# A matmul with subtraction on one core: 16 rows to a partition, another list of transfers, and eleven pairs of tiles transposed on VectorE

## The chip, the core and the metric

The kernel runs on one core of a Trainium2 chip. The metric is the device time in microseconds (us). The kernel before takes 211.34 us (median of eight runs, 210.97 to 211.55).

## What is computed

```python
# x: (16, 512, 1024), weight: (1024, 768), sub_value: (16, 512, 768), all float32
out = (np.matmul(x, weight) - sub_value).astype(np.float32)
```

Flattened, x has 8,192 rows of 1,024 numbers, and output and sub_value have 8,192 rows of 768.

## The kernel before

**Tiles.** The rows are worked in 64 m tiles of 128 rows. A tile doesn't hold 128 rows that follow each other: with `S = 8`, a group of 1,024 rows gives each of the 128 partitions a run of eight rows that lie together in memory, and m tile `mi` is row `mi % 8` of every run of group `mi // 8`. A transfer of n tiles of one group so moves, for each partition, one run of n rows: n x 4,096 bytes of x, or n x 3,072 bytes of sub_value or output.

**Rings.** x lands in a ring of 16 tiles (`x_ring`), sub_value in a ring of 32 (`so_ring`). The result is written over sub_value in place and stored from there. The weight comes in four chunks of 256 of its rows, each through two slots of `so_ring` (slots 24 to 31), from where VectorE (DVE) casts it to float16 (L112).

**Transfers.** All are issued by SyncE (SP), in the order of the list `TRANSFERS`: (kind, first tile, number of tiles), with x, w, s (sub_value) and o (output). `issue()` (L91) takes the head of the list as soon as, in the program's order, what it needs has been written down: for x, the casts of the tiles whose slots it takes; for s, the stores that free its slots; for o, the subtractions. On the chip SP then waits at each issue for those instructions or transfers to have ended, and what is behind in the list waits with it. In the trace the ninth issue also waits for the first transfer to land, the tenth for the second, and so on.

**The work of a tile.**

- ScalarE (ACT) casts x to float16: L135, or L132 for tiles of a pair that DVE will transpose.
- Transpose, by one of two ways. On TensorE (PE): four transposes against the identity (L144; two float16 numbers travel as one float32), then a copy out of PSUM by ACT (L151). On DVE, for the pairs that begin at a tile in `ON_DVE`: 16 stream transposes of 32 x 256 for a pair (L165), no PE and no copy.
- PE: sixteen matmuls of 128 x 128 by 384 columns (L177), into one of three PSUM buffers.
- DVE subtracts sub_value and writes the result (L189, `finish`), which frees the PSUM buffer.

**Order.** Written out by hand. The head (L214 to L242) works tiles 0 to 2 chunk by chunk as the weight arrives, with filler matmuls on zeros between (`idle`, L205). Then the loop over `mi` (L246): tile `mi`'s matmuls, with the PE transposes of tile `mi + 2` between them, then the casts of tiles that are due (four tiles ahead, or seven for a DVE pair), then `finish(mi)`, then up to four waiting DVE transposes. The 16 transposes of a pair join the waiting ones six tiles before the pair and so are spread over four tiles.

```python
    for mi in range(HEAD, n_mt):
        t = mi + TA
        tr = transposes(t) if t < n_mt and t - t % 2 not in ON_DVE else []
...
        finish(mi)
        if mi + LEAD_DVE - 1 in ON_DVE:
            waiting += transposes_dve(mi + LEAD_DVE - 1)
        for f in waiting[:PER]:
            f()
```

Of the kernel before, what the change touches and what calls it, by code (L numbers as in the profile page):

```python
# [10 lines left out]
F32 = mybir.dt.float32  # L11
F16 = mybir.dt.float16

S = 8
NX, NSO = 16, 32
TA = 2
CA = 2
LEAD_DVE = 7
PER = 4
HEAD = 3  # L20
ON_DVE = frozenset(range(18, 60, 6))

TRANSFERS = [
    ('x', 0, 1), ('w', 0, 1), ('x', 1, 1), ('w', 1, 1), ('x', 2, 1), ('w', 2, 1),
    ('w', 3, 1), ('x', 3, 2), ('s', 0, 1), ('x', 5, 3), ('s', 1, 3), ('x', 8, 3),
    ('s', 4, 4), ('x', 11, 5), ('s', 8, 8), ('x', 16, 8), ('x', 24, 3), ('s', 16, 8),
    ('x', 27, 5), ('o', 0, 8), ('s', 24, 8), ('x', 32, 8), ('s', 32, 8), ('o', 8, 8),
    ('x', 40, 8), ('s', 40, 8), ('x', 48, 8), ('o', 16, 8), ('o', 24, 8), ('s', 48, 8),
    ('x', 56, 8), ('s', 56, 8), ('o', 32, 8), ('o', 40, 8), ('o', 48, 8), ('o', 56, 4),
    ('o', 60, 2), ('o', 62, 1), ('o', 63, 1),  # L30
]


# [1 line left out]
def kernel(  # L35
# [20 lines left out]

    x_s = x_flat.rearrange("(s p j) k -> s p j k", p=P, j=S)
    sub_s = sub_flat.rearrange("(s p j) n -> s p j n", p=P, j=S)
    out_s = out_flat.rearrange("(s p j) n -> s p j n", p=P, j=S)
    w_c = weight.rearrange("(c p r) n -> c p r n", p=P, r=2)  # L60

    def rows(view, mi, n):
        return view[mi // S][:, mi % S : mi % S + n]

# [26 lines left out]
    def issue():  # L91
        while todo:
# [24 lines left out]
            here = ring[:, at % size : at % size + n]  # L117
            there = view[at // S][:, at % S : at % S + n]
            if kind == "o":
# [4 lines left out]
    def cast(mi):  # L124
        assert mi in done["x"]
        done["cast"].add(mi)
        x_in = x_ring[:, mi % NX]
        first = mi - mi % 2
        if first in ON_DVE:
            if mi == first:  # L130
                x16_t["pair", mi] = x16p_pool.tile([P, 2, K], F16, name="x16p_tile")
            keep(nc.scalar.copy(out=x16_t["pair", first][:, mi - first], in_=x_in))  # L132
        else:
            x16_t[mi] = x16_pool.tile([P, K], F16, name="x16_tile")
            keep(nc.scalar.copy(out=x16_t[mi], in_=x_in))  # L135
        issue()


    def transposes(mi):
        def one(c):  # L140
            def f():
                if c == 0:
                    ps_t[mi] = psum_t_pool.tile([P, K], F16, name="psum_t")
                keep(nc.tensor.transpose(  # L144
                    ps_t[mi].bitcast(F32)[:, c * P : (c + 1) * P],
                    x16_t[mi].bitcast(F32)[:, c * P : (c + 1) * P],
                    ident,
                ))
                if c == n_c - 1:
                    xt_t[mi] = xt_pool.tile([P, K], F16, name="xt_tile")  # L150
                    keep(nc.scalar.copy(out=xt_t[mi], in_=ps_t.pop(mi)))  # L151
                    x16_t.pop(mi)
            return f
        return [one(c) for c in range(n_c)]

    def transposes_dve(mi):

        x16 = x16_t.pop(("pair", mi)).bitcast(F32).rearrange("p j (c q) -> p (j c) q", c=n_c)
        xt_p = xtp_pool.tile([P, 2, K], F16, name="xtp_tile")
        xt_t[mi], xt_t[mi + 1] = xt_p[:, 0], xt_p[:, 1]  # L160
        xt = xt_p.bitcast(F32).rearrange("p j (c m) -> p (j c) m", c=n_c)

        def one(a, b):
            def f():
                keep(nc.vector.transpose(  # L165
                    xt[b * Q : (b + 1) * Q, :, a * Q : (a + 1) * Q],
                    x16[a * Q : (a + 1) * Q, :, b * Q : (b + 1) * Q],
                ))
            return f
        return [one(a, b) for a in range(P // Q) for b in range(P // Q)]  # L170
# [14 lines left out]
    def finish(mi):  # L185
        assert mi in done["s"]
        done["finish"].add(mi)
        o = so_ring[:, mi % NSO].rearrange("p (h n) -> p h n", h=2)
        keep(nc.vector.tensor_tensor(  # L189
            out=o, in0=po_t.pop(mi)[:, :, :NS], in1=o, op=mybir.AluOpType.subtract  # L190
        ))
        issue()
# [10 lines left out]
    def idle(n):  # L203
        for _ in range(n):
            keep(nc.tensor.matmul(idle_o[:, 0], idle_w, idle_x, start=True, stop=True))  # L205

    def lead(mi):
        return LEAD_DVE if mi - mi % 2 in ON_DVE else TA + CA

# [1 line left out]
        for f in transposes(mi):  # L211
            f()

    idle(13)  # L214
    cast(0)
    transpose_tile(0)
    idle(5)
# [28 lines left out]
# [3 lines that stand above are left out]
        for c in range(n_c):  # L249
# [6 lines left out]
# [3 lines that stand above are left out]
# [34 lines left out]
```

## Time and profile before

| | before |
|---|---|
| median of 8 runs | 211.34 us |
| the profiled execution | 211.03 us |
| its span | 209.2 us |
| granted TensorE clock, mean | 0.998 |
| PE busy | 198.3 us (95%) |
| DVE busy | 114.1 us (55%) |
| ACT busy | 112.8 us (54%) |
| PE waits in all, longest releaser | 2.7 us on the cast (L135) |
| last subtraction ends | 205.1 us |

The span runs from the first to the last instruction of the program; the device time has some 1.8 us more. Times of events are counted from the span's start. Busy shares say how long an engine had an instruction in work, not which engine sets the end: for that one looks at what each stage waits for. The DMA row of the page is the mean busy share of the 16 DMA engines that carry every transfer. A transfer's time to landing runs from its issue on SP to its last byte's completion, and so holds the time that it stands behind earlier transfers.

### The profile page before, as it was taken

The numbers are of one execution on the slowest core, as the hardware profiler recorded it, in microseconds if no ns is written. First come the engines' busy times: TensorE is split into PE (matmuls) and PEld (weight loads), VectorE is DVE, ScalarE is ACT, GpSimd is POOL, SyncE is SP. The second block draws the span as 40 slices with busy tenths as digits, with TensorE's granted clock in tenths as the row PEclk, the third lists the DMA queues.
The fourth block names the chain that finished last, engine by engine and source line by source line (L and its number), as shares of the span: only waits on it lengthen the run. The fifth ranks groups of instructions, "written<-read, shape, count | busy, mean of one in ns | idle before, by whom it ended". The sixth has DMA issues, their size and how long they took to land.

```text
span 209.2 us, 2967 instructions
## 1 busy us (share of the span) xinstructions
PE 198.3 (95%) x1249; PEld 130.4 (62%) x1249; DVE 114.1 (55%) x186; ACT 112.8 (54%) x115; POOL 0.7 (0%) x6
## 2 busy tenths in 40 slices
PE   7997799999989999999999999999999999999990
PEld 3464467667656566667667666667666766767650
DVE  0342044206149759929947955982993795333231
ACT  3555665675496193555727629456473750765410
POOL 1000000000000000000000000000000000000000
PEclk9999999999999999999999999999999999999999
DMA  6999999999999999999999999999999999999994
GB/s 220 420 429 422 427 431 436 441 436 439 387 451 418 436 442 407 464 420 418 440 415 440 434 423 443 432 415 421 432 442 445 420 421 423 431 423 428 432 390 186
DMA packets 5629, 87.22 MB, mean 417 GB/s; under 512 B 624, under 2 KB 624, under 8 KB 2032
## 3 DMA queue, kind: packets, MB, share of 16 engines
q1 hardware_dynamic: 5616, 87.03, 97.8%
q8 instruction: 10, 0.16, 0.3%
q14 instruction: 3, 0.02, 0.0%
HBM read 61.87 MB, written 25.17 MB: 416 GB/s over the span
## 4 chain that ended last, share of the span: by engine, by line
PE 68%; DMA 20%; ACT 4%; DVE 3%; SPq 2%; issue 1%
PE psum_o L177 60%; DMA x_ring<-in_x_dram 20%; PE psum_t L144 8%; ACT x_tile L135 2%; DVE xtp_tile L165 2%; ACT xt_tile L151 1%; DVE so_ring L189 1%; SPq L110 1%; SPq L122 1%; ACT x16p_tile L132 0%
## 5 line engine op out<-in xcount | busy, mean ns | idle before, releaser
L177 PE MATMUL psum_o<-w_sb,xt_tile 128*128 128x384 f16 x800 | 145.7, 326 | 1.2 <-ACT xt_tile L151 1.0
L177 PEld LDWEIGHTS <-xt_tile 128*128 128x128 f16 x800 | 78.2, 98 | 41.0 <-ACT xt_tile L151 1.8
L189 DVE TENSOR_TENSOR so_ring<-psum_o,so_ring 128x768 f32<-128x768 f32 x64 | 60.7, 956 | 61.4 <-PE psum_o L177 41.2
L151 ACT COPY xt_tile<-psum_t 128x1024 f16<-128x1024 f16 x50 | 50.6, 1012 | 73.6 <-PE psum_t L144 72.8
L165 DVE STREAM_TRANSPOSE xtp_tile<-x16p_tile 32x256 f32<-32x256 f32 x112 | 48.8, 436 | 18.2 <-ACT x16p_tile L132 16.5
L144 PE MATMUL psum_t<-ident,x_tile 128*128 128x128 f32 x200 | 52.3, 274 | 3.0 <-ACT x_tile L135 2.7
L135 ACT CAST x_tile<-x_ring 128x1024 f16<-128x1024 f32 x50 | 51.6, 1049 | 6.3 <-DMA x_ring<-in_x_dram 6.3
L177 PE MATMUL psum_o<-w_sb,xtp_tile 128*128 128x384 f16 x224 | 42.9, 326 | 0.3 <-DVE xtp_tile L165 0.3
L144 PEld LDWEIGHTS psum_t<-ident,x_tile 128*128 128x128 f32 x200 | 27.7, 141 | 17.0 <-ACT x_tile L135 5.0
L177 PEld LDWEIGHTS <-xtp_tile 128*128 128x128 f16 x224 | 21.8, 98 | 10.4 <-DVE xtp_tile L165 0.7
L132 ACT CAST x16p_tile<-x_ring 128x1024 f16<-128x1024 f32 x14 | 14.6, 1046 | 6.5 <-DMA x_ring<-in_x_dram 6.5
L205 PE MATMUL psum_o<-idle_x,idle_w 128*128 128x512 f16 x25 | 8.8, 508 | 1.3 <-DVE idle_x L200 1.3
L112 DVE CAST w_sb<-so_ring 128x768 f16<-128x768 f32 x8 | 4.1, 556 | 10.6 <-DMA so_ring<-in_weight_dram 10.6
L205 PEld LDWEIGHTS <-idle_w 128*128 128x128 f16 x25 | 3.1, 122 | 4.9 <-issue 3.2
L135 ACT ACT_TABLE_LOAD x1 | 1.3, 1283 | 0.7 <-PEq L277 0.7
L199 DVE MEMSET idle_w<- 128x64 uint32 x1 | 0.1, 112 | 0.8 <-PEq L277 0.8
masks.py:199 POOL TENSOR_SCALAR_AFFINE_SELECT ident<-ident 128x128 f32<-128x128 f32 x1 | 0.3, 292 | 0.1
L200 DVE MEMSET idle_x<- 128x256 uint32 x1 | 0.3, 272 | 0.0
masks.py:197 POOL MEMSET ident<- 128x128 f32 x1 | 0.2, 205 | 0.3 <-POOLq L277 0.3
L277 POOL MEMSET const-bfloat16-1.0<- 128x1 bf16 x1 | 0.1, 101 | 0.0
L277 POOL MEMSET const-uint8-127<- 128x1 uint8 x1 | 0.1, 101 | 0.0
L277 POOL MEMSET const-float32-0.0<- 128x1 f32 x1 | 0.1, 99 | 0.2 <-issue 0.2
(1 smaller groups left out, 0.1 us busy)
## 6 DMA issues: line engine op xcount, KB each, us to landing
so_ring<-in_sub_value_dram SPq DMA_DIRECT2D x7, 3072.0 KB, 24.7
out_dram<-so_ring SPq DMA_DIRECT2D x7, 3072.0 KB, 31.2
x_ring<-in_x_dram SPq DMA_DIRECT2D x5, 4096.0 KB, 22.9
x_ring<-in_x_dram SPq DMA_DIRECT2D x2, 2560.0 KB, 23.1
x_ring<-in_x_dram SPq DMA_DIRECT2D x3, 1536.0 KB, 19.4
so_ring<-in_weight_dram SPq DMA_DIRECT2D x4, 768.0 KB, 8.8
x_ring<-in_x_dram SPq DMA_DIRECT2D x3, 512.0 KB, 6.3
so_ring<-in_sub_value_dram SPq DMA_DIRECT2D x1, 1536.0 KB, 21.8
```

What stands on the lines that cost most here:

```text
L110: keep(nc.sync.dma_start(out=st, in_=w_c[at]))
L112: keep(nc.vector.tensor_copy(out=w_sb[:, at, r], in_=st[:, r]))
L122: keep(nc.sync.dma_start(out=here, in_=there))
L132: keep(nc.scalar.copy(out=x16_t["pair", first][:, mi - first], in_=x_in))
L135: keep(nc.scalar.copy(out=x16_t[mi], in_=x_in))
L144: keep(nc.tensor.transpose(ps_t[mi].bitcast(F32)[:, c * P : (c + 1) * P], x16_t[mi].bitcast(F32)[:, c * P : (c + 1) * P], ident,))
L151: keep(nc.scalar.copy(out=xt_t[mi], in_=ps_t.pop(mi)))
L165: keep(nc.vector.transpose(xt[b * Q : (b + 1) * Q, :, a * Q : (a + 1) * Q], x16[a * Q : (a + 1) * Q, :, b * Q : (b + 1) * Q],))
L177: keep(nc.tensor.matmul(po_t[mi][:, h, :NS], xt_t[mi][:, 2 * P * c + r : 2 * P * (c + 1) : 2], w_sb[:, c, r, h * NS : (h + 1) * NS], start ...
L189: keep(nc.vector.tensor_tensor(out=o, in0=po_t.pop(mi)[:, :, :NS], in1=o, op=mybir.AluOpType.subtract))
L205: keep(nc.tensor.matmul(idle_o[:, 0], idle_w, idle_x, start=True, stop=True))
L277: nc = _bacc.Bacc("TRN2", target_bir_lowering=False, num_devices=1)
```

## The change

Four things in one diff:

- `S` goes from 8 to 16: groups of 2,048 rows, each partition holding a run of 16. Transfers may now be up to 16 tiles long, and their runs up to 49,152 bytes. The rows of one m tile lie 64 KB apart in x instead of 32 KB, in sub_value and output 48 KB instead of 24 KB.
- The list of transfers is another: 34 entries instead of 39. Weight chunk 0 goes first, ahead of x tile 0. Sub_value starts with tiles 0 to 5 in one transfer (before: tile 0, then 1 to 3, then 4 to 7). The stores are of 16, 12, 4, 16, 7, 6, 2 and 1 tiles.
- `ON_DVE` holds eleven pairs, from tile 12 to tile 55, most of them four tiles apart, instead of seven pairs six tiles apart (18 to 55).
- Sixteen filler matmuls instead of 13 before the first cast.

```diff
-S = 8
+S = 16
 NX, NSO = 16, 32
 TA = 2
 CA = 2
 LEAD_DVE = 7
 PER = 4
 HEAD = 3
-ON_DVE = frozenset(range(18, 60, 6))
+ON_DVE = frozenset((12, 16, 20, 24, 28, 32, 38, 42, 46, 50, 54))
 
 TRANSFERS = [
-    ('x', 0, 1), ('w', 0, 1), ('x', 1, 1), ('w', 1, 1), ('x', 2, 1), ('w', 2, 1),
-    ('w', 3, 1), ('x', 3, 2), ('s', 0, 1), ('x', 5, 3), ('s', 1, 3), ('x', 8, 3),
-    ('s', 4, 4), ('x', 11, 5), ('s', 8, 8), ('x', 16, 8), ('x', 24, 3), ('s', 16, 8),
-    ('x', 27, 5), ('o', 0, 8), ('s', 24, 8), ('x', 32, 8), ('s', 32, 8), ('o', 8, 8),
-    ('x', 40, 8), ('s', 40, 8), ('x', 48, 8), ('o', 16, 8), ('o', 24, 8), ('s', 48, 8),
-    ('x', 56, 8), ('s', 56, 8), ('o', 32, 8), ('o', 40, 8), ('o', 48, 8), ('o', 56, 4),
-    ('o', 60, 2), ('o', 62, 1), ('o', 63, 1),
+    ('w', 0, 1), ('x', 0, 1), ('x', 1, 1), ('w', 1, 1), ('x', 2, 1), ('w', 2, 1),
+    ('w', 3, 1), ('x', 3, 3), ('s', 0, 6), ('x', 6, 3), ('x', 9, 7), ('s', 6, 5),
+    ('x', 16, 6), ('s', 11, 5), ('s', 16, 6), ('x', 22, 10), ('x', 32, 4), ('s', 22, 10),
+    ('o', 0, 16), ('x', 36, 4), ('s', 32, 5), ('x', 40, 8), ('s', 37, 11), ('x', 48, 8),
+    ('o', 16, 12), ('o', 28, 4), ('s', 48, 7), ('x', 56, 8), ('s', 55, 9), ('o', 32, 16),
+    ('o', 48, 7), ('o', 55, 6), ('o', 61, 2), ('o', 63, 1),
 ]
...
-    idle(13)
+    idle(16)
     cast(0)
     transpose_tile(0)
```

## The prediction

> **What bounds the kernel now.** I read the 40 slices of the page first, then the DMA queues, the issues with their times to landing, and the chain last.
>
> Page, parts 2 and 3 (busy tenths of the 16 DMA engines, GB/s moved; packets, MB, share):
>
> ```profile
> DMA  6999999999999999999999999999999999999994
> GB/s 220 420 429 422 427 431 436 441 436 439 387 451 418 436 442 407 464 420 418 440 415 440 434 423 443 432 415 421 432 442 445 420 421 423 431 423 428 432 390 186
> ...
> q1 hardware_dynamic: 5616, 87.03, 97.8%
> ```
>
> From the second slice to the last but one the DMA engines never rest, and 87.03 MB is what has to move: x 33.55, weight 3.15, sub_value and output 25.17 each. A landing is the issue time plus the time to landing. The load of m tiles 24-31 of sub_value lands at 87.87, the load of x 32-39 behind it at 97.59: 4.19 MB in 9.72 us, 431 GB/s. That pace holds to the end. The last two stores, from the DMA view of a window around each (KB, us to landing):
>
> ```profile
> out_dram<-so_ring SPq DMA_DIRECT2D x1, 384.0 KB, 4.9
> ```
>
> ```profile
> out_dram<-so_ring SPq DMA_DIRECT2D x1, 384.0 KB, 3.2
> ```
>
> The first is issued at 202.51 and lands at 207.4, the second at 205.11 and 208.3: 0.9 us apart, just the time of its bytes (eight packets of 3,072 bytes an engine, 0.121 us each in the trace's packet records, 0.97). So the last store hardly waited for its late issue; the slowest engine was still behind.
>
> PE looks like the bound too. The chain in order of time ends so:
>
> ```profile
> 198.88 5.21 PE psum_o L177 x32
> 204.12 0.96 DVE so_ring L189
> ```
>
> From 60 us to 204 it is nearly all PE at L177. **Two limits end together**: the data (208.3) and PE, then DVE at L189, then the last store (204.1 + 1.0 + 3.2 = 208.3). A gain must come from both; PE's alone is worth nothing.
>
> **DVE transposes and PE.** From the groups (count, busy us, mean ns):
>
> ```profile
> L165 DVE STREAM_TRANSPOSE xtp_tile<-x16p_tile 32x256 f32<-32x256 f32 x112 | 48.8, 436 | 18.2 <-ACT x16p_tile L132 16.5
> L144 PE MATMUL psum_t<-ident,x_tile 128*128 128x128 f32 x200 | 52.3, 274 | 3.0 <-ACT x_tile L135 2.7
> ```
>
> Eleven pairs for seven take eight m tiles from PE: 32 transposes fewer. One costs PE less than its 274 ns, which overlap: in the chain four matmuls with a transpose begin every 0.76 us, and 36 without take 5.85, or 0.65 for four. So 32 x 0.11 = **3.5 us off PE**; ACT loses 8 copies of 1.012 us (L151), 8.1 us, unneeded there (busy 54%). DVE gains 64 transposes, 28 us. The timeline of DVE shows its pace (start, duration):
>
> ```profile
> 60.08 1.78 DVE L165 STREAM_TRANSPOSE xtp_tile<-x16p_tile 32x256 f32<-32x256 f32 x4 [5.03 <-ACT x16p_tile L132]
> 61.90 0.96 DVE L189 TENSOR_TENSOR so_ring<-psum_o,so_ring 128x768 f32<-128x768 f32 x1
> 62.88 1.78 DVE L165 STREAM_TRANSPOSE xtp_tile<-x16p_tile 32x256 f32<-32x256 f32 x4
> ```
>
> A subtraction and four transposes repeat every 2.80 us. Pairs are now four tiles apart instead of six, so DVE works without pause, 4 x 2.80 = 11.20 us a pair, where PE needs 2 x 3.04 + 2 x 2.60 = 11.28. It fits by 0.08 us; time that DVE loses to a late sub_value tile comes back only at the six-tile step from 32 to 38 and after the last pair.
>
> **The head.** Weight chunk 0 goes ahead of x tile 0 on SP's queue: x 0 lands 0.79 MB / 0.429 = 1.8 us later (4.8 becomes 6.7), and the cast, transposes and first matmuls on ACT and PE move by about 1.1 us. From x 1 on the bytes ahead are the same. The three added fillers cost 0.75 to 1.3 us (0.25 or 0.44 each in the timeline), while PE waits for x 0 anyway. All this is covered: PE must then wait for x 3, now in a transfer of three tiles, until about 18.7 (17.4 before). Next late is sub_value: tiles 0-5 come as one transfer ending at 8.65 MB, where before 8.91 MB had landed at 25.6: about 25.0. The subtraction of tile 0 is done at 26.0, and only then is one of three output banks free for tile 3, which ends at 29.1 instead of 26.7: **+2.4 us on PE**. Later, x 9-15 (13.89 MB) land near 37.2, just in time for the transposes beside tile 7 (38.2). Sub_value 6-10 (15.86 MB) lands at 41.9 and holds DVE 3.7 us, so pair 12's transposes end at 41.9 + 11.2 = 53.1 where tile 12 is due at 52.5: a stall of 0.6. Before, PE lost 2.2 us near 57, 59 and 70, where x 16-23 landed at 56.2, after their casts were due; now x 16-21 land at 49 and x 22-31 at 71, needed by PE at 53 and 76, so these waits go. Beyond this sub_value comes in time or under 1 us late, inside the slack of three banks.
>
> PE's end: 204.1 + 2.4 + 0.6 - 2.2 - 3.5 = 201.4. The last subtraction ends at 202.4, the last store is issued 2.7 us earlier than now. So PE leaves the path; **the DMA engines stay**.
>
> **The transfers.** The packet records give 8 data packets and one of 4 bytes an engine for every transfer (39 x 144 = 5,616). Median durations: 121 ns for 3,072 bytes, 912 for 24,576, 1,213 for 32,768. The slope is 36.7 ns a KB (1,000 bytes), the fixed part 9 ns; the 4-byte packet also takes 9. A transfer thus costs 9 x 9 = 81 ns beyond its bytes, and 34 instead of 39 save 5 x 81 = **0.4 us**. No other fixed cost is seen between transfers: 8 x 1.213 + 0.009 is the 9.71 us that landings are apart.
>
> The page "DMA: Bandwidth & Descriptors" of the Trainium skill (Bandwidth, Measured) gives a fixed cost of about 2 us a DMA; five fewer would then save 10 us, which the back-to-back landings here rule out.
>
> What could leave a DMA engine idle? SP issues in order, and two loads of sub_value wait for a store to land: tiles 32-36 for output 0-15, tiles 48-54 for output 16-27. Queued behind each store is only x 36-39 (2.10 MB, 4.9 us) or output 28-31 (1.57 MB, 3.7 us); before, it was 3.15 to 7.34 MB. An issue needs 4.1 - 1.3 = 2.8 us beside its own bytes (x 0) or 3.2 - 1.0 = 2.2 (the last store). Both are under 3.7, so the cost is nothing; even if the whole 4.1 of x 0 were needed, it would be 0.4. The large x transfer 22-31 waits for the cast of tile 15, which stands behind tile 11's matmuls and so is done near 53.5, while the data queued before it last to 59 (23.33 MB); x 32-35 wait for tile 19's, behind tile 15, near 65.4, against 71 (28.57 MB).
>
> No row has a packet above 32,768 bytes; five transfers now have runs of 33,792 to 49,152. If cut in two, they add at most 5 x 8 x 9 ns = 0.36 us; if not, nothing. I take nothing, as the fixed part is flat from 3,072 to 32,768. No row has rows spaced 64 KB (x) or 48 KB: the spacings of 6 KB (weight), 24 and 32 KB lie on one line within 1%. That bounds it to 1% of 203 us, 2.0 us, either way; I take nothing.
>
> The same page (Latency and other measured facts, on HBM row pitch) speaks against the change: at a pitch of 512 KiB it has 207 GB/s against 214, and half at 4 MiB. It states nothing for 64 KiB; its 3% would be 6 us.
>
> **Sum.** 211.03 of the profiled execution (span 209.2, 1.8 around it) less 0.4 is 210.6; the shown median is 0.3 above that execution, so I set 211.34 - 0.4 = **210.9**. Chance moves it by about as much: the trace holds ten 16 KB instruction fetches of about 1.0 us, each delaying one engine, and one landing's lag of the last engine behind the first grew from 0.93 to 1.69 us at the first of them. Measurement tells 0.2%, 0.42 us, from no change.
>
> **Rivals.**
> - *The saving doesn't show* (0.18): runs are cut (-0.4 + 0.36), or an extra fetch or a store wait gives 0.4 back. 211.3. For it: unseen sizes; against: the flat fixed part.
> - *A fetch misses the slowest engine* (0.07): 0.6 more is saved, 210.3. The first one shows what is at stake.
> - *Wider row spacing slows packets* (0.10), the slower side: in every x, sub_value and output transfer, every 1% is 2.0 us, so that 1% gives 211.34 + 2.0 - 0.4 = 212.9. It decides from 0.4%, 0.8 us. Against it: three spacings on one line.
> - *DVE becomes the bound* (0.05): with 0.08 us to spare a pair, lateness beyond the computed one pushes PE one for one. The store before the last would land near 206.9 and an issue needs 2.8, so the last one may be issued up to 204.1, 1.7 later than computed; 3 us of lateness give 210.9 + 1.3 = 212.2.
>
> **Numbers.** The forecast case has 0.60, from 210.4 to 211.3: 0.40 faster, 0.20 within. Faster: 0.40 + 0.07 = 0.47. Same: 0.20 + 0.18 = 0.38. Slower: 0.10 + 0.05 = 0.15. The range 210.1 to 212.2 takes in the first three cases and the milder part of the last two.
>
> **What would show it.** Right: DMA tenths full to the last slice, 4,896 packets on q1, the chain's last subtraction near 202.4 with the last store's time to landing 2 to 3 us longer, DVE without gaps between 42 and 110 us. Wrong: a slice below 9 near 102 or 152 (store waits), 24 KB packets off 0.912 us (spacing), more than 4,896 packets (cut runs), or PE waiting at L177 for xtp_tile again and again (DVE).

## The result, and the profile after

The changed kernel takes **213.16 us** (median of 11 runs, 212.34 to 215.0) against 211.18 for the kernel before (31 runs beside them): a ratio of 1.0102, with an interval of 1.0087 to 1.0117. It is 1% slower, where 0.2% faster was forecast, and outside the range. Some executions fall into a slower state, and the ratios leave those out, so that a ratio need not be the quotient of the two medians beside it. The profiled execution is one of 213.18 us, with a span of 211.4.

The kernel after, parts 2 and 3 of the page (a slice is 5.285 us; slice 14 is 68.7 to 74.0, slices 19 and 20 are 95.1 to 105.7, slices 29 and 30 are 148.0 to 158.6, slice 34 is 174.4 to 179.7):

```profile
DMA  6999999999999899998999999999999999999993
GB/s 216 380 429 441 423 461 401 448 416 423 469 418 446 381 451 460 437 437 377 390 451 415 449 438 418 405 439 443 376 402 451 437 416 388 452 440 394 431 409 143
...
q1 hardware_dynamic: 4896, 87.03, 97.4%
```

The same bytes go in 4,896 packets instead of 5,616, as computed. But the DMA engines are not full any more: slices 14 and 19 have an 8, and the bytes dip in slice 14 (381), 19 and 20 (377, 390), 29 and 30 (376, 402) and 34 (388). In the kernel before the slices of the same numbers have 436, 418 and 440, 432 and 442, 423. A dip that lasts is a debt: each byte that isn't moved is moved at the end. Not every dip lasts, since a packet of up to 49,152 bytes counts in one slice alone; the lags below tell which do.

The end of the chain of waits, in order of time, and the waits of SP's queue (line waited for: us in total, times, longest):

```profile
118.85 32.65 DMA out_dram<-so_ring
151.52 10.15 DMA so_ring<-in_sub_value_dram
...
197.35 5.21 PE psum_o L176 x32
202.59 0.96 DVE so_ring L188
```

```profile
SPq L121 <- DMA out_dram<-so_ring: 58.7, 3, 31.8
```

The last subtraction ends at 203.55; before, it ended at 205.1. So PE and DVE are 1.5 us earlier, and the kernel still ends later. The chain now runs through the store of output 16-27, which lands at 151.50, and the load of sub_value 48-54, which SP issues only then, at 151.52. The stores at the end, in the DMA view of the last microseconds (KB, us from issue to landing):

```profile
out_dram<-so_ring SPq DMA_DIRECT2D x1, 768.0 KB, 8.5
out_dram<-so_ring SPq DMA_DIRECT2D x1, 384.0 KB, 6.8
```

The last store is issued at 203.57 and lands at 210.4. Before, it was issued at 205.1 and needed 3.2. The 3.6 us more are time behind other stores: **the data alone sets the end, and it is 2.1 us late** (210.39 against 208.28).

To see where it got late I read the packet records of the trace. A transfer is cut into 16 parts, one for each DMA engine, and each part has its own landing. From every landing I take the time that the packets of all transfers so far need on an engine without a pause (36.74 ns a KB of 1,000 bytes and 9 ns a packet). What is left is the engine's **lag**. An engine that always has work keeps its lag, but for up to 0.1 us that it falls at each store; a pause or a late packet raises it. Lag of the fastest and the slowest of the 16 engines (us), at the landing of the transfer with the tile that is named:

| landing of | before | after |
|---|---|---|
| the load of x 32 | 2.36, 4.30 | 2.96, 5.46 |
| the load of sub_value 32 | 2.37, 4.52 | 3.20, 5.36 |
| the store of output 27 | 2.24, 4.67 | 3.39, 6.20 |
| the store of output 31 | 2.24, 4.67 | 3.35, 6.15 |
| the load of sub_value 48 | 2.15, 4.62 | 4.74, 6.28 |
| the load of sub_value 63 | 2.23, 5.04 | 5.08, 7.92 |
| the last store | 4.22, 5.25 | 4.89, 7.78 |

The account closes with this: the packets' own time is 0.40 us less, as forecast, the slowest engine's lag 2.53 us more, together 2.13 (2.11 measured). And it shows four things. The 16 engines don't run in step: the slowest is most of the time some 2 to 3 us behind the fastest. Of the 2.5 us, 1.16 are there before any load waits for a store (first row: 4.30 against 5.46). At the load of sub_value 48-54, the **fastest** one jumps by 1.4 us while the slowest hardly moves: the engines that were ahead have lost their lead. And some 15 us after that load landed, at 176.7 to 177.6 us, 15 packets, about one an engine, are 0.14 to 1.33 us late, and the slowest lag goes to 7.9. The mean lag of the 16 engines says which dips last: it rises by 0.55 us between the landings of x 32-35 and x 40-47 (slices 19 and 20), by 0.78 between output 28-31 and x 56-63 (slices 29 and 30) and by 0.46 at sub_value 55-63 (slice 34), where the kernel before has 0.05 to 0.07 each, but by 0.16 alone over x 22-31 (slice 14), as in e12 (0.15), which has no dip there.

### The profile page after: what moved, and what is told of

Its sections match the earlier page's. It is cut to its first block, busy times and chain, and to the rows that moved or that the text cites. A ratio compares the mean times of both kernels' runs of the same rounds, so it can differ in the third digit from the quotient of the medians.

```text
span 211.4 us, 2953 instructions
## 1 busy us (share of the span) xinstructions
PE 195.9 (93%) x1220; PEld 126.7 (60%) x1220; DVE 141.2 (67%) x250; ACT 104.8 (50%) x107; POOL 0.7 (0%) x6
## 3 DMA queue, kind: packets, MB, share of 16 engines
q1 hardware_dynamic: 4896, 87.03, 97.4%
## 4 chain that ended last, share of the span: by engine, by line
PE 56%; DMA 32%; DVE 7%; ACT 1%; issue 1%; DVEq 0%
PE psum_o L176 50%; DMA out_dram<-so_ring 15%; DMA so_ring<-in_sub_value_dram 14%; PE psum_t L143 5%; DVE xtp_tile L164 4%; DVE so_ring L188 3%; DMA so_ring<-in_weight_dram 2%; ACT xt_tile L150 0%; ACT x16p_tile L131 0%; ACT x_tile L134 0%; DVEq L188 0%
## 5 line engine op out<-in xcount | busy, mean ns | idle before, releaser
L176 PE MATMUL psum_o<-w_sb,xt_tile 128*128 128x384 f16 x672 | 120.0, 329 | 2.2 <-DVE so_ring L188 2.1
L176 PEld LDWEIGHTS <-xt_tile 128*128 128x128 f16 x672 | 66.1, 99 | 40.1 <-issue 3.2
L150 ACT COPY xt_tile<-psum_t 128x1024 f16<-128x1024 f16 x42 | 42.5, 1012 | 77.9 <-PE psum_t L143 77.5
L164 DVE STREAM_TRANSPOSE xtp_tile<-x16p_tile 32x256 f32<-32x256 f32 x176 | 76.6, 435 | 4.8 <-ACT x16p_tile L131 2.1
L176 PE MATMUL psum_o<-w_sb,xtp_tile 128*128 128x384 f16 x352 | 67.4, 326 | 0.1
L134 ACT CAST x_tile<-x_ring 128x1024 f16<-128x1024 f32 x42 | 43.8, 1047 | 14.9 <-DMA x_ring<-in_x_dram 14.9
L143 PE MATMUL psum_t<-ident,x_tile 128*128 128x128 f32 x168 | 43.8, 275 | 3.1 <-ACT x_tile L134 2.9
L176 PEld LDWEIGHTS <-xtp_tile 128*128 128x128 f16 x352 | 34.4, 98 | 15.7 <-DVE xtp_tile L164 0.5
L143 PEld LDWEIGHTS psum_t<-ident,x_tile 128*128 128x128 f32 x168 | 23.2, 142 | 14.6 <-ACT x_tile L134 3.5
L131 ACT CAST x16p_tile<-x_ring 128x1024 f16<-128x1024 f32 x22 | 23.0, 1046 | 0.1
```

The lines of the kernel that those rows point to most:

```text
L143: keep(nc.tensor.transpose(ps_t[mi].bitcast(F32)[:, c * P : (c + 1) * P], x16_t[mi].bitcast(F32)[:, c * P : (c + 1) * P], ident,))
L164: keep(nc.vector.transpose(xt[b * Q : (b + 1) * Q, :, a * Q : (a + 1) * Q], x16[a * Q : (a + 1) * Q, :, b * Q : (b + 1) * Q],))
L176: keep(nc.tensor.matmul(po_t[mi][:, h, :NS], xt_t[mi][:, 2 * P * c + r : 2 * P * (c + 1) : 2], w_sb[:, c, r, h * NS : (h + 1) * NS], start ...
```

## The experiments

Three causes were open: the rows' wider spacing (S = 16), the new list of transfers (loads that are issued too late to keep the engines fed), and the eleven DVE pairs (their traffic disturbs transfers). Each run was taken beside the kernel before, which had 210.90 to 211.00 us. Ratios are to the kernel before, and the measured numbers come together here:

| run | us | ratio (interval) |
|---|---|---|
| e1: before, S = 16 | 211.59 | 1.0028 (1.0017 to 1.0040) |
| e2: after, S = 8, transfers cut to fit | 211.89 | 1.0044 (1.0032 to 1.0057) |
| e3: list of e2, S = 16 | 212.27 | 1.0061 (1.0049 to 1.0073) |
| e4: before, eleven pairs | 214.16 | 1.0155 (1.0137 to 1.0173) |
| e5: after, both large stores cut | 211.56 | 1.0031 (1.0012 to 1.0050) |
| e6: e2 with late stores | 213.89 | 1.0119 (1.0092 to 1.0146) |
| e7: after, x 0 first | 213.38 | 1.0092 (1.0056 to 1.0128) |
| e8: after, once more | 212.73 | 1.0088 (1.0061 to 1.0114) |
| e9: after, only the first store cut | 212.92 | 1.0088 (1.0060 to 1.0116) |
| e10: after, only the second store cut | 212.87 | 1.0087 (1.0054 to 1.0121) |
| e11: e5 with x 0 first | 211.31 | 1.0036 (1.0016 to 1.0055) |
| e12: e11 with x 22-31 cut | 211.25 | 1.0014 (1.0005 to 1.0022) |
| e13: before, one late store | 211.92 | 1.0052 (1.0034 to 1.0070) |
| e14: e12, tiles 0-15 in runs of 8 | 210.94 | 1.0000 (0.9992 to 1.0009) |

### e1 to e4: one part of the change at a time

**e1**, the kernel before with only the spacing changed:

```diff
-S = 8
+S = 16
```

> The kernel before with S = 16 and nothing else: same list of 39 transfers, same pairs, same order; only the rows of a tile lie 64 KB (x) and 48 KB (sub_value, output) apart, and a transfer of eight tiles takes half of every run. Theory A (the wider spacing makes packets late, most of all the short ones of the head and those where several engines meet): 212.2 to 213.5 us, with x 1 and x 2 packets above 0.159 us near 4 to 10 us. Rival B (the new list, with stores that loads wait for and cold starts at 102 and 152 us, loses the time): 210.9 to 211.5, no change. Rival C (eleven pairs on VectorE disturb the transfers): no change here either.

The spacing alone costs 0.28%, 0.6 us: real, and not enough.

**e2**, the kernel after with S = 8. A transfer can't cross a group of eight tiles then, so ten are cut in two (44 transfers), the large stores among them (the fences from here on show only the entries of the list that change):

```diff
-S = 16
+S = 8
...
-('x', 6, 3), ('s', 6, 5), ('x', 22, 10), ('s', 22, 10)
+('x', 6, 2), ('x', 8, 1), ('s', 6, 2), ('s', 8, 3), ('x', 22, 2), ('x', 24, 8), ('s', 22, 2), ('s', 24, 8)
-('o', 0, 16), ('s', 37, 11), ('o', 16, 12), ('s', 55, 9), ('o', 32, 16), ('o', 55, 6)
+('o', 0, 8), ('o', 8, 8), ('s', 37, 3), ('s', 40, 8), ('o', 16, 8), ('o', 24, 4)
+('s', 55, 1), ('s', 56, 8), ('o', 32, 8), ('o', 40, 8), ('o', 55, 1), ('o', 56, 5)
```

> The changed kernel with S = 8 again; its transfers are cut where they cross a group of eight tiles (44 instead of 34), the order of the bytes, the pairs and the fillers stay. Theory A (spacing): back to 211 to 211.8, since ten transfers more cost 10 x 0.08 = 0.8 us beside the 34 and 0.4 beside the 39 of before. Rival B (order, store waits): stays at 213 or above. Rival C (DVE pairs): stays at 213 or above.

**e3**, the list of e2 with `S = 16` kept:

> The same list of 44 cut transfers as in the run with S = 8, now with S = 16: nothing differs between these two but the addresses. Theory A (spacing): 1.0 to 2.5 us above its twin, so 212.5 to 214. Rival B and C: equal to its twin within 0.4 us. If long packets (up to 49,152 bytes) were the trouble, this one would be faster than the changed kernel.

e3 still has the wide spacing and ten more transfers than the kernel after, and is 0.4% faster than it (0.3% by e8 below). Ten transfers more cost 0.8 us or 0.4% by the packets' fixed time, so that some 0.7 to 0.8 of the 1% goes away by cutting transfers. Which of the cuts does it, these two runs can't say: they also ease both store waits. Between e2 and e3 only the spacing differs: 0.17%, with intervals that just overlap.

**e4**, the kernel before with the eleven pairs:

```diff
-ON_DVE = frozenset(range(18, 60, 6))
+ON_DVE = frozenset((12, 16, 20, 24, 28, 32, 38, 42, 46, 50, 54))
```

> The kernel before with the eleven pairs of the changed one, nothing else. Theory A (spacing) and B (order): 210.8 to 211.4, no change beyond 0.2%, since the transfers set the end and PE only gets earlier; its last subtraction ends 2 to 4 us earlier. Rival C (eleven pairs disturb the transfers): 212 or more.

It is slower than anything else, but not by disturbed transfers. Its chain ends in PE and DVE, and its waits have PE at the transposes (us in total, times, longest):

```profile
202.94 5.21 PE psum_o L177 x32
208.18 0.96 DVE so_ring L189
```

```profile
PEld psum_t L144 <- ACT x_tile L135: 9.2, 6, 3.6
PE psum_t L144 <- ACT x_tile L135: 6.7, 4, 3.2
...
PEld L177 <- ACT xt_tile L151: 2.9, 2, 2.4
```

The last subtraction ends at 209.1. With the old list x 16-23 come in one transfer and land near 56, while the eleven pairs want the casts of tiles 16 and on earlier: from 40 to 62 us PE is idle for 4.7 us (1.1 in the kernel before), and the granted clock is 0.79 from 40 to 48 and 0.76 from 56 to 62 (1.00 there). The slowest lag before the last stores is 5.6, close to the 5.5 of the kernel before. So no disturbed transfers show in this trace; what it shows is PE waiting for x and at a lower clock. My expectation missed since it left this wait out.

### e5 to e8: the large stores

**e5**, the kernel after with both large stores cut, two transfers more:

```diff
-('o', 0, 16)
+('o', 0, 8), ('o', 8, 8)
...
-('o', 16, 12)
+('o', 16, 8), ('o', 24, 4)
```

> The changed kernel with two stores cut: output 0-15 into 0-7 and 8-15, output 16-27 into 16-23 and 24-27 (36 transfers). The loads of sub_value 32-36 and 48-54 then wait for a store that lands 5 to 7 us earlier, with 5.2 and 3.1 MB queued behind it. Theory B (the wait for the slowest engine's part of a store leaves the fast engines dry, pulls them back to the slowest and makes all of them meet at the same places afterwards): 211.6 to 212.4 us, 1 us below the changed kernel, the engines' landings of one transfer 2.5 to 3.5 us apart at the end with the fastest early, no group of late packets near 104 and 152 us. Theory A (64 KB spacing alone): within 0.3 us of the changed kernel.

It takes 211.56 us. By the ratios 0.71% is gone of the 1.02% (of 0.88% by e8, 0.57%), some 1.2 to 1.5 us. The two loads of sub_value wait for output 0-4 and 16-22 to be stored, which the first half now brings. SP's timeline of e5 (start, duration):

```profile
93.58 0.34 SPq L121 DMA_DIRECT2D so_ring<-in_sub_value_dram  x1
...
146.97 0.34 SPq L121 DMA_DIRECT2D so_ring<-in_sub_value_dram  x1
```

and of the kernel after:

```profile
100.92 0.33 SPq L121 DMA_DIRECT2D so_ring<-in_sub_value_dram  x1
...
151.52 0.34 SPq L121 DMA_DIRECT2D so_ring<-in_sub_value_dram  x1
```

The loads go out 7.3 and 4.6 us earlier, and the fastest engine's lag stays at 2.8 to 3.0 from 101 to 179 us, with the slowest at 5.1 to 5.3. Six packets near 155 us are late by up to 1.01 us here too, but neither end of the 16 moves.

**e6**, the contrary: e2, which has S = 8 and no large store, with the halves of the stores in the other order, so that the loads wait for the second one. No byte, packet or transfer differs:

```diff
-('o', 0, 8), ('o', 8, 8)
+('o', 8, 8), ('o', 0, 8)
...
-('o', 16, 8), ('o', 24, 4)
+('o', 24, 4), ('o', 16, 8)
```

> The run with S = 8 and 44 transfers, with the two stores that loads wait for moved behind the other half (output 8-15 ahead of 0-7, 24-27 ahead of 16-23), so that again only 2.10 and 1.57 MB cover the waits, as in the changed kernel. Theory B alone: 1 us above the run with S = 8, about 212.9, with late packets near 104 and 152 us. If the wait hurts only together with the 64 KB spacing: 211.9 to 212.2, as without the wait.

It takes 2.0 us more than e2, 213.89 against 211.89 (0.75% by the ratios), twice what I expected, and so is no faster than the kernel after. The stretches of e6 (columns: length; busy time of PE, PEld, DVE, ACT and POOL with counts; granted clock; DMA share; GB/s):

```profile
150.00:152.00 2.00, 2.00 (x15) 1.38 (x14) 1.92 (x4) 0.00 (x0) 0.00 (x0) 1.00 0.90 381
152.00:154.00 2.00, 2.00 (x16) 1.41 (x14) 1.93 (x5) 1.01 (x1) 0.00 (x0) 1.00 1.03 379
154.00:156.00 2.00, 2.00 (x14) 1.36 (x13) 1.93 (x5) 0.39 (x1) 0.00 (x0) 1.00 0.93 363
...
178.00:180.00 2.00, 2.00 (x15) 1.42 (x14) 0.20 (x1) 0.92 (x2) 0.00 (x0) 1.00 0.80 320
```

the same of e2:

```profile
152.00:154.00 2.00, 2.00 (x16) 1.39 (x14) 1.94 (x4) 1.01 (x1) 0.00 (x0) 1.00 1.07 458
154.00:156.00 2.00, 2.00 (x15) 1.35 (x14) 1.90 (x6) 0.59 (x1) 0.00 (x0) 1.00 1.00 430
176.00:178.00 2.00, 2.00 (x15) 1.41 (x14) 0.35 (x1) 1.46 (x2) 0.00 (x0) 1.00 0.98 418
178.00:180.00 2.00, 2.00 (x15) 1.41 (x14) 0.96 (x1) 1.46 (x2) 0.00 (x0) 1.00 1.03 442
```

and of the kernel after:

```profile
152.00:154.00 2.00, 2.00 (x15) 1.40 (x14) 1.92 (x4) 0.70 (x1) 0.00 (x0) 1.00 1.04 364
154.00:156.00 2.00, 2.00 (x15) 1.39 (x13) 1.94 (x4) 0.31 (x1) 0.00 (x0) 1.00 1.03 404
176.00:178.00 2.00, 2.00 (x15) 1.35 (x14) 0.96 (x1) 1.87 (x2) 0.00 (x0) 1.00 1.04 332
```

e6 and the kernel after miss bytes in the same two places, within 2 us, and e2 doesn't. (In the second the kernel before has a thin stretch too, 381 in 176 to 178.) PE is busy throughout in all three, so nobody waits for these bytes yet; only the end shows them. (The share of a stretch can be over 1.00, since a packet counts where it is recorded; the GB/s are the better column.) In e6's records the fastest lag goes from 2.97 at the store of output 31 to 4.45 at the load of sub_value 48, as in the kernel after.

**e7**, the kernel after with x 0 first again and the old fillers:

```diff
-('w', 0, 1), ('x', 0, 1)
+('x', 0, 1), ('w', 0, 1)
...
-    idle(16)
+    idle(13)
```

> The changed kernel with x tile 0 ahead of weight chunk 0 and 13 fillers, as before. Theory: the order of the first two transfers is worth nothing, within 0.4 us of the changed kernel; if the weight-first head gave away the 0.5 us by which the slowest engine is later after 10 us, it is 0.5 us faster.

**e8**, the kernel after unchanged, for another profile of it:

> The changed kernel as it is, on the chip of the three others. It tells whether the late packets near 104, 136, 152 and 177 us come at the same places in another execution: theory B expects those at 104 and 152 again, right behind the two waits; if the ones near 136 and 177 are chance, they move or go.

e7 at 1.0092 and e8 at 1.0088 can't be told apart: the order in the head is worth nothing that shows in the time. The profile of e8 is of its longest execution (215.69 us, with a median of 212.73), so it isn't read here, and whether the late packets of the kernel after come at the same places again stays open by this run.

### e9 to e12: which of the late loads

**e9** cuts only the store of output 0-15, **e10** only that of 16-27, as in e5:

> The changed kernel with only output 0-15 cut into 0-7 and 8-15: the wait of sub_value 32-36 is eased, that of sub_value 48-54 on output 16-27 (3.7 us of transfers behind it) stays. Theory B in the form that the second wait does the harm (the engines' landings of one transfer shrink to 1.5 us apart there, and each execution seen so far with that has a group of late packets near 177 us): 212.4 to 213.2. If the first wait does it: 211.3 to 211.8.

> The changed kernel with only output 16-27 cut into 16-23 and 24-27: the wait of sub_value 48-54 is eased (3.1 MB behind it), that of sub_value 32-36 (4.9 us of transfers behind it) stays. If the second wait does the harm: 211.4 to 212.0, no group of late packets near 177 us. If the first: 212.4 or above.

**e11** is e5 with e7's head:

> Both stores cut and x tile 0 first with 13 fillers: what is left of the change are the 64 KB spacing, the list and the eleven pairs. The run with both cut was at 1.0031 of the kernel before, as much as S = 16 alone gave (1.0028). If spacing is all that is left, 1.002 to 1.004 again, less 0.24 us for three transfers fewer; if the weight-first head had a part, 211.0 to 211.3. It is also the nearest candidate to beat the kernel before: that needs 210.5 or less.

**e12** is e11 with the third load cut that waits with little behind it, the one that waits for the cast of tile 15:

```diff
-('x', 22, 10)
+('x', 22, 5), ('x', 27, 5)
```

> The run with both stores cut and x first, with the third late load eased too: x 22-31 cut into 22-26 (which needs the casts to tile 10 only, done near 42 us) and 27-31 (37 transfers). The run before it had two kinds of executions, near 211.1 and near 212.45; in the two profiles where x 22-31 was issued at 55 to 56 us instead of 53.7, groups of late packets came near 57 to 83 us already. Theory B in its general form (a load issued later than about 3 us before the fastest engine runs dry bunches the engines): the slower kind goes, 210.8 to 211.3 throughout. If the two kinds have another cause, they stay.

Cutting one store alone brings nothing that shows (1.0088 and 1.0087), cutting both brings 0.6%. e9 is plain: its load of sub_value 48 still goes out at 150.60, and slice 29 has 397. e10 I had expected near e5, and it missed. SP's timeline of e10 has the reason in the head of the list:

```profile
56.00 0.33 SPq L121 DMA_DIRECT2D x_ring<-in_x_dram  x1
```

and the same issue in e12:

```profile
53.55 0.33 SPq L121 DMA_DIRECT2D x_ring<-in_x_dram  x1
```

In e10, x 22-31 were issued 2.3 us later than in the kernel after (53.68), because the cast of tile 15 ended at 55.97 instead of 53.66; its slice 14 has 352. The first packets of x 22-31 start at 57.2 in both, so e10 had 1.2 us from the issue where the kernel after had 3.6. From then on e10 has packets late by over 0.13 us in three groups, 10 at 57 to 59 us, 14 at 68 to 73 and 28 at 80 to 84, and the mean lag rises by 1.33 us to the landing of sub_value 22-31, where the kernel after has 0.15. So x 22-31 is a third place of the same kind, with a cover that this kernel sometimes has and sometimes not. The cast was late because PE, on which it waits in the program's order, was late since the head: in e10 sub_value 0-5 landed at 25.99 (24.58 in the kernel after), and the granted clock was 0.50 from 26 to 30 us and 0.70 from 30 to 34 (0.61 and 1.00). That these two make up the 2.3 us is not tested. The late x 22-31 fits the spread of e11, whose 12 runs fall into two heaps near 211.1 and 212.45; e12 has the load in two and one heap (210.80 to 211.81). That e11's slower heap is late at x 22-31 isn't shown, as its profile is one of the faster heap. e12's page:

```profile
DMA  6999999999999999999999999999999999998993
GB/s 217 393 434 432 416 458 412 453 414 416 434 436 435 415 443 431 438 408 425 432 449 432 440 419 433 421 433 411 418 457 443 437 421 469 441 435 368 420 417 147
```

All the dips named above are gone: 415, 425 and 432, 418 and 457, 469. (Slice 37, 368, lies in the large stores at the end; there one engine alone falls back, from 5.0 to 5.8, and in e5 one to 6.6. A 16 KB instruction fetch starts in that store in both, at 186.6 and 187.3.)

### e13 and e14: both ways once more

**e13** puts one late load into the kernel before, by the order of three stores (one transfer more, 0.08 us), so that 1.57 MB instead of 3.15 are behind the store that the load of sub_value 48 waits for:

```diff
-('o', 16, 8), ('o', 24, 8)
+('o', 24, 4), ('o', 16, 8), ('o', 28, 4)
```

> The kernel before with one thing changed: its stores of output 16-31 in another order and cut (24-27, then 16-23, then 28-31; 40 transfers), so that the load of sub_value 48-55 waits for a store behind which only 1.57 MB are queued. Bytes, pairs, spacing and head are those of before. Theory B: 0.08 us for the transfer more, and 0.7 to 1.7 us for the bunched engines, so 211.7 to 212.7, with a group of late packets near 152 to 156 us and another in the load that follows. Rival (bunching harms only in the changed kernel's long transfers or spacing): 210.8 to 211.2.

It costs 0.52% (1.1 us). The load is issued at 149.87, where the kernel before has 146.66. The fastest lag rises from 2.41 (store of output 31) to 2.65 with ten packets late by up to 0.87 us, then to 3.33 with some 22 late at 174 to 177 us, and the slowest from 4.1 to 5.2; it goes on to 6.5 at the store of output 32-39, where a fetch at 182.9 delays one engine. That last step is partly chance; the six times, all above the 17 of the kernel before beside them, are not. So neither S = 16, nor long packets, nor the eleven pairs are needed for the loss.

**e14** is e12 with the first 16 tiles in runs of eight rows, as before the change, and the transfers cut to fit (39 of them):

```diff
+    x_s8 = x_flat.rearrange("(s p j) k -> s p j k", p=P, j=8)
...
+            view, run = (view[1], 8) if at < 16 else (view[0], S)
+            there = view[at // run][:, at % run : at % run + n]
...
-('x', 6, 3), ('x', 9, 7), ('s', 6, 5)
+('x', 6, 2), ('x', 8, 2), ('x', 10, 6), ('s', 6, 2), ('s', 8, 3)
```

> The run with all three late loads eased, with the first 16 tiles in runs of 8 rows as before and only the rest in runs of 16 (39 transfers, as many as before; x 6-8 and 9-15 go as 6-7, 8-9 and 10-15, sub_value 6-10 as 6-7 and 8-10). If the last 0.3 us of that run come from the short loads of the head, whose packets are late at 64 KB spacing (x 1 and x 2: 0.2 us a transfer) and not at 32 KB, this one is at 210.8 to 211.1, equal to the kernel before within 0.1%, and the engines' lag behind their packets' own time at 20 us is back at 2.5 to 3.5 us. If not, it stays at 1.001 to 1.003. To beat the kernel before by more than can be told from no change it would need 210.5, which neither theory gives.

It is at 1.0000 (0.9992 to 1.0009), 0.14% under e12 with two transfers more. The two transfers are worth 0.16 us or 0.08%, so the shorter runs of the first 16 tiles bring about 0.2%, near what e1 and e3 give for the spacing as a whole. The intervals of e12 and e14 just overlap, so this points to the head and doesn't prove it. In the packet records of the kernel after, single packets of 4,096 bytes of x 1 are late by up to 0.36 us, in the kernel before and e14 none by 0.05. But the spacing isn't alone in this: e2 and e6, at 32 KB with the weight first, have them too (up to 0.31). The mean lag at the last weight chunk has both: 2.81 to 3.00 us at 32 KB with x 0 first (before, e4, e13, e14), 3.16 to 3.22 at 64 KB with x 0 first (e1, e7, e11, e12), 3.03 and 3.22 at 32 KB with the weight first (e2, e6), 3.33 to 3.41 with both (after, e3, e5, e9, e10). The slowest lag near 18 us is 3.98 after, 3.50 before and 3.08 in e14. No version was faster than the kernel before.

## Why the prediction was wrong

**Two limits, and the data as the one that stays:** right at the end. PE's gain is there and worth nothing: the last subtraction ends 1.5 us earlier. But PE wasn't out of it: its time in the head decides whether x 22-31 go out in time (e10).

**DVE and PE:** right in the main. In the kernel after, DVE repeats every 2.80 us (start, duration):

```profile
42.07 0.96 DVE L188 TENSOR_TENSOR so_ring<-psum_o,so_ring 128x768 f32<-128x768 f32 x1 [4.57 <-DMA so_ring<-in_sub_value_dram]
42.95 1.77 DVE L164 STREAM_TRANSPOSE xtp_tile<-x16p_tile 32x256 f32<-32x256 f32 x4
44.75 0.96 DVE L188 TENSOR_TENSOR so_ring<-psum_o,so_ring 128x768 f32<-128x768 f32 x1
```

The first of these waits for sub_value 6-10, which landed at 41.98 where 41.9 was forecast; tiles 0-5 landed at 24.6 (forecast 25.0). The last subtraction ends at 203.55, 1.1 later than the forecast 202.4, still before the data. The forecast took its paces from the kernel before, at full clock; from 26 to 30 us the granted clock was 0.61, and PE ran 18 matmuls where it ran 28 in the next 4 us. Whether that is the 1.1 is not shown.

**The saving of the transfers:** right in the packets (4,896; nothing extra for runs of 33,792 to 49,152 bytes, which go as single packets on the same line), and so 0.40 us of the engines' time. e14, with the count of before, equals it. (The page that the prediction set against this has its 2 us a DMA not under Bandwidth, Measured, but in its anatomy of one DMA, as a fit for transfers that GpSimd issues; SP issues those here.)

**The step that failed** is the one headed "What could leave a DMA engine idle?", with its sentence "Both are under 3.7, so the cost is nothing". It set 4.9 and 3.7 us of queued bytes against the 2.2 to 2.8 that an issue needs. But the load is issued when the store's **slowest** engine has landed, and the queue that is left counts for the **fastest**, which is 2.4 to 2.8 us further on. What is left to it is 4.9 - 2.4 = 2.5 us and 3.7 - 2.8 = 0.9 us (queue less the spread at the landing that the load waits for). The first is at the edge, and the fastest lag rose by 0.3 there; the second is short by 1.3 to 1.9, and the fastest lag rose by 1.4. The prediction even had the spread in a row (0.93 to 1.69 us, read in the head) and used it for chance alone. Even that reading, "if the whole 4.1 of x 0 were needed, it would be 0.4", had the wrong size: as long as only the fast engines pause, the end should not move at all. That the slowest lose too is what makes the 2 us.

**Why the slow engines lose** is not settled. What the traces show is a company: in the kernel after, e6, e7, e9 and e13, whose load of sub_value 48 goes out only when a store has landed with nothing but output 28-31 behind it, the engines close up and then, between 150 and 178 us, have late packets together: 32 to 41 are late by over 0.13 us there, up to 1.7 us each. In e2, e3, e11, e12 and e14 it is 1 to 4, in e5 7, in the kernel before 9. The first wait has a like trace: at 134 to 142 us 5 to 19 packets are late in the kernel after, e6, e7 and e10, whose load of sub_value 32 is late, and none or one in e2, e3, e5, e9, e11, e12 and e14, which have it early. That the late issue causes the loss is shown, by e5 and e12 (taken away) and e6 and e13 (put in). That it does so by engines in step asking the same memory at once is only a guess; no run tried it. (The Trainium skill, "DMA: Bandwidth & Descriptors", Latency and other measured facts, gives streams in lock step that meet in one memory channel as its own unverified inference for slow pitches; here the loss is there at 32 KB too, in e6 and e13.)

**The wide spacing** was taken as nothing, with 2.0 us either way: it is 0.6 us (e1) or 0.4 (e3 against e2), inside the bound and as much as the 0.4 that the change saves, or more. Its rival, "every 1% is 2.0 us" in every transfer, gave 212.9, near the result, by the wrong way: long runs at the wide spacing stay on the line (24,576 bytes take 0.912 us in e1 too), and what cost there is points to the short loads of the head.

**What would show it** was named well: a dip near 102 or 152 for the store waits. In the tenths it came at the first alone (slice 19, an 8); at the second they stay at 9 and only the bytes dip (376, 402). And the same shortage came, in e10, in a place that the prediction had looked at and let go (x 22-31, "while the data queued before it last to 59": for the fastest engine, to 57).

**The sum**, in shares of the kernel before: late loads behind the stores 0.6 to 0.7% (after and e8 against e5), x 22-31 0.2% (e11 against e12), spacing 0.14 to 0.28%, five transfers fewer -0.2%. These add up to 0.7 to 1.0, where 0.88 to 1.02 was measured for the kernel after.

## What to carry to other kernels

A queue that looks full by the landings of whole transfers can be empty for its fastest engine: when a load waits for a store, reckon what is queued behind the store, take off the spread of the engines' landings, and only then compare with the time that an issue needs. A larger store saves some packets' fixed time (0.08 us a transfer here), but it turns "my slots are free" into "the whole store has landed"; cut it where a load waits for its first part. The same goes for a load that waits for an engine's work, such as a cast: its cover is gone when that engine is late (2.3 us in e10). And work taken off an engine is worth nothing while the transfers end no earlier, so look at the bytes per slice before and after first.

## What the runs showed of the hardware

- The 16 DMA engines that share every transfer drift apart: by 0.3 to 1.2 us in the first transfer, by 2.1 to 4.1 us near 190 us. Instruction fetches of 16 KB, about one every 20 us and 0.9 to 1.1 us long, come with one packet each that is 0.33 to 0.66 us late; about the first one, near 22 to 24 us, the slowest lag rises by 0.2 to 1.7 us. An engine that is behind doesn't catch up with the others as long as the queue is full: in e2 the slowest is 3.0 us behind the fastest at 73 us and 3.6 at 200.
- A run of 49,152 bytes goes as one packet, within 0.01 us of the line through the shorter ones.
- Packets of 4,096 bytes of x 1 are late by up to 0.53 us where their rows are 64 KB apart (e5), by up to 0.31 at 32 KB with the weight first (e6), and none by over 0.08 at 32 KB with x 0 first (e4).
- After a stretch in which PE had waited (slices 4 and 5 of the kernel after), the granted clock is half for 3.4 us (25.7 to 29.1), with a mean of 0.981, and for 6.8 us in e10; e12 has such a stretch too and full clock there, so I draw no rule from it.
